# A two-layer encoder on one core: the clocks that give out weight splits follow each element, the fourth product of the seven goes onto the seventh's bank, the last block turns later, and two load slots are added

## The chip, the cores and the metric

The kernel runs on one core of one Trainium2 chip. The metric is device time in microseconds (us) of one execution, and less is better. Five engines work side by side, each through its own list of instructions in order: TensorE (PE: matmuls and transposes), VectorE (DVE), ScalarE (ACT), GpSimd (POOL) and SyncE (SP, which here starts nearly all transfers from memory). They wait for each other by semaphores.

## The reference

Two layers, each of three steps; after each step the sum with the step's input is normalised over 1024 features. The first and third steps are a gated feed-forward network (FFN), so there are four of these. The middle step is a bidirectional mLSTM in the first layer and a windowed attention in the second. All is float32, for 256 rows (two groups of 128, called t=0 and t=1).

```python
def swiglu(x, w_in, w_out):
    gu = x @ w_in                                   # (256,1024) @ (1024, 2*2816)
    g, u = gu[..., :D_FF], gu[..., D_FF:]
    return (jax.nn.silu(g) * u) @ w_out             # (256,2816) @ (2816,1024)

def reference(x, ffn_w_in, ffn_w_out, ln_g, ln_b, ...):
    for l in range(DEPTH):                          # DEPTH = 2
        x = layer_norm(ALPHA*x + 0.5*swiglu(x, ffn_w_in[l,0], ffn_w_out[l,0]), ln_g[l,0], ln_b[l,0])
        y = mlstm_mixer(x, ...) if l == 0 else window_attention(x, ...)
        x = layer_norm(ALPHA*x + y, ln_g[l,1], ln_b[l,1])
        x = layer_norm(ALPHA*x + 0.5*swiglu(x, ffn_w_in[l,1], ffn_w_out[l,1]), ln_g[l,2], ln_b[l,2])
    return x
```

## The kernel before

**Three matmuls for one.** Each float32 operand is split into a high part in TensorE's own format (`w_hi`, `xT_hi`) and the rest (`w_lo`, `xT_lo`); a product is hi*hi + hi*lo + lo*hi (`mm3`). So every piece of weights that arrives, 128 x 1024 numbers or 512 KB, is split before it is used: ACT casts the high part (`high`, "CAST w_hi"), DVE subtracts it from the raw piece (`low`, "TENSOR_TENSOR w_lo"). RING = 10 pieces can be split ahead of their use.

**An FFN.** The 2816 hidden columns go in blocks. First 512 columns "wide" (x is the stationary operand, the weights stream), then GROUPS = 3 groups, each of 256 columns "narrow" (the weights are stationary) and 512 columns whose gate and up-projection are made together in `seven`, a scheme of seven products instead of eight on 2 x 2 blocks. Its products use sums of x blocks (S1 to S4, made once by `x_sum`) and sums of weight blocks, which are made in place on DVE ("TENSOR_TENSOR s_raw") or by a transfer that adds onto what lies there (POOL, L204). Each product is 12 matmuls of 512 columns (`product`) onto a PSUM bank, and a closing function (`end1` to `end7`) takes the result out: copies on ACT (tile `e`), additions, subtractions and multiplications on DVE (tiles `e`), SiLU on ACT. `u0` and `u1` are the hidden values of t=0 and t=1; `tr` transposes them on TensorE ("MATMUL pw<-ident,e") and splits the result into `h_hi` and `h_lo` for the down-projection `down`, one row of 128 hidden columns of `w_out` at a time (12 matmuls "py").

Before the change the order in a group is: products 1 (bank qa), 2 (qc), a `down`, product 5 with S1 (qb), product 6 with S2 (onto qa, which is copied out first: `e1`), a `down`, product 3 with S4 (onto qb, copied out first as `e5`; `end3` makes `u0` by a subtraction and a multiplication), product 7 with S3 (onto qa, copied out first as `e2`; `end7` copies `e3` and subtracts into `u1`), in the first two groups a `down`, `tr` of `u0`, product 4 onto a fresh bank qd (`end4`: addition, SiLU, multiplication into `u1`), in the first two groups a `down`. The first two groups are "full"; the third, the last block, has no `down` at these two places. `tr` of `u1` comes in the middle of the next group's first narrow half, or, for the last block, inside `tail`.

**The end of an FFN.** `tail` does the last six down rows, first for t=0 and then for t=1, each in two halves of 512 columns, and norms each t as its sums are ready (`Norm.half`: "SCALAR_TENSOR_TENSOR x" and "BN_STATS"; `Norm.finish`: multiply by `ln_g`, add `ln_b`). `ln_g` and `ln_b` are loaded to two fixed tiles when g == 1.

**Transfers and slots.** A raw piece goes to one of 4 slots (`w_raw`), the blocks of `seven` that are summed to one of 6 more that exist only in an FFN (`s_raw`). A load is issued as soon as the instruction that frees its slot has been written, so SP waits for the DVE split that read the slot last.

**Who is given what, when.** In an FFN the planner `Paced` counts rough clocks (in ns) while the program is written: one for TensorE, one for DVE, one for ACT, one for transfers. After each matmul `fill` looks whether ACT or DVE is less than AHEAD = 900 ns ahead of TensorE's clock and, if the piece has been there for SOON (-600: 600 ns), writes one more split or sum into that engine's list. An engine's clock starts an instruction no earlier than its own clock and TensorE's; what other engines' results it needs is not followed, but for three tables of times of raw pieces and of their halves. So this planner's constants and costs set how many splits stand ahead of each `end` function in DVE's and ACT's lists. In the mixers the numbers of splits are written by hand.

All that goes through the planner's wrapper stands under L79 in the profile, so instructions are known by tiles: "w_hi", "w_lo", "e", "h_lo" and so on.

Of the kernel before, what the change touches and what calls it, by code (L numbers as in the profile page):

```python
# [1 line left out]

# [21 lines left out]
S_RAW = 6  # L24
RING = 10
# [11 lines left out]
AHEAD = 900.0  # L37
SOON = -600.0
LANDING = 2200.0
LOADING = 1340.0  # L40
ADDING = 8000.0


class Paced:
# [3 lines left out]
    def __init__(self, nc):  # L48
        self.nc = nc
        self.pe = self.vec = self.act = self.dma = 0.0  # L50
        self.filler = None
# [7 lines left out]
    def on_vector(self, name, n):  # L59
        self.vec = max(self.vec, self.pe) + (n + 71) / 0.96  # L60

    def on_scalar(self, name, n):
        self.act = max(self.act, self.pe) + n * 0.912 + 25

    def on_tensor(self, name, n):
        self.pe += 109.0 if name == "transpose" else n / 2.4 + 13.3
# [4 lines left out]
class Engine:  # L71
# [3 lines left out]
    def __getattr__(self, name):  # L75
        f = getattr(self.engine, name)

        def call(out, *args, **kw):
            r = f(out, *args, **kw)  # L79
            n = 1  # L80
            for d in getattr(out, "shape", (1, 1400))[1:]:
                n *= d
            self.told(name, n)
# [4 lines left out]
class Weights:  # L88
# [5 lines left out]
    def __init__(self, nc, pool, words, plan, after):  # L94
        self.nc, self.pool, self.words, self.plan, self.after = nc, pool, words, plan, after
        self.raw, self.parts, self.half, self.sums = {}, {}, [], []
        self.at, self.high_at, self.low_at = {}, {}, {}
        self.made = self.used = self.room = 0
        self.todo = {tag: [i for i, w in enumerate(words) if w["tag"] == tag] for tag in ("w_raw", "s_raw")}
        self.free = {"w_raw": RAW_BUFS, "s_raw": 0}  # L100
# [9 lines left out]
    def open(self, pool, end):  # L110

        self.spool, self.send = pool, end
        self.free["s_raw"] = S_RAW
        self.load()

    def load(self, most=None):
        nc = self.nc
        for tag, most_ in (("w_raw", most), ("s_raw", 1 if most is None else most)):
            n = 0
            while self.todo[tag] and self.free[tag] and (most_ is None or n < most_):  # L120
                i = self.todo[tag][0]
                if tag == "s_raw" and i >= self.send:
                    break
                pool = self.pool if tag == "w_raw" else self.spool
                t = pool.tile([128, D], F32, name=tag, tag=tag, bufs=RAW_BUFS if tag == "w_raw" else S_RAW)
                nc.sync.dma_start(t.rearrange("p (k f) -> p k f", k=self.words[i]["k"]), self.words[i]["src"])
                nc.dma = max(nc.dma, nc.pe + LANDING) + LOADING
                self.raw[i], self.at[i] = t, nc.dma
                self.free[tag] -= 1
# [3 lines left out]
    def drop(self, w):  # L133
        self.uses[w] -= 1
        if not self.uses[w]:
            del self.raw[w]
            self.free[self.words[w]["tag"]] += 1
# [7 lines left out]
    def high(self):  # L145
# [11 lines left out]
        nc.act = max(nc.act, self.at[p["word"]])  # L157
# [9 lines left out]
        self.high_at[i] = nc.act  # L167
# [3 lines left out]
    def low(self):  # L171
# [6 lines left out]
        nc.vec = max(nc.vec, self.high_at[i])  # L178
# [9 lines left out]
        self.low_at[i] = nc.vec  # L188
# [4 lines left out]
    def sum(self):  # L193
# [3 lines left out]
        if isinstance(v, int):  # L197
            nc.vec = max(nc.vec, self.at[w], self.at[v])
            nc.vector.tensor_add(t, t, self.raw[v])
            self.at[w] = nc.vec  # L200
            self.drop(v)
            self.load()
        else:
            nc.gpsimd.dma_start(t.rearrange("p (k f) -> p k f", k=self.words[w]["k"]), v, accum_op=OP.add)  # L204
            self.at[w] = max(nc.vec, nc.pe) + ADDING

    def fill(self):

        nc = self.nc
        while True:  # L210
            act, vec = max(nc.act, nc.pe), max(nc.vec, nc.pe)
            if act < nc.pe + AHEAD and len(self.half) < 2 and self.made < min(self.room, len(self.plan)):
                p = self.plan[self.made]
                if (p["word"] in self.raw and self.at[p["word"]] < act + SOON
# [3 lines left out]
            if vec < nc.pe + AHEAD:  # L218
                if self.half and self.high_at[self.half[0][0]] < vec + SOON:
                    self.low()  # L220
                    continue
                if self.sums and max(self.at[w] for w in self.sums[0][1:] if isinstance(w, int)) < vec + SOON:
# [4 lines left out]
    def take(self, n):  # L227
# [3 lines left out]
        self.nc.pe = max([self.nc.pe] + [self.low_at[j] for j in range(i, i + n)])  # L231
# [27 lines left out]
def trunk_kernel(ctx: ExitStack, tc: tile.TileContext, x, ffn_w_in, ffn_w_out, ln_g, ln_b, ml_w_in, ml_gate_b,  # L259
# [37 lines left out]
    def seven(w, c0, c1, downs):  # L297
# [70 lines left out]
    def load_x(t, h):  # L368
        s_ = slice(h * 512, h * 512 + 512)
        nc.sync.dma_start(xt[t][:, s_], x[0, t * 128:(t + 1) * 128, s_])  # L370
# [77 lines left out]
    def load_ln(l, n):  # L448
        t = []
        for name, w in (("g", ln_g), ("b", ln_b)):  # L450
            a = state.tile([128, D], F32, name="ln_" + name, tag="ln_" + name)
# [59 lines left out]
    def ffn(l, i, n, pending, last):  # L511
        with ExitStack() as ph:
# [3 lines left out]
            def h_room(width):  # L516
                return tuple(pool.tile([128, width, S], FR, name="h" + e, tag="h" + e, bufs=3) for e in ("_hi", "_lo"))
# [760 lines left out]
```

## Time and profile before

| | |
|---|---|
| time, three runs | 967.67 us median (964.8 to 967.9) |
| the profiled execution | 966.85 us, span of its instructions 965.1 us |
| TensorE | 931.9 us busy (97%), 4938 matmuls |
| DVE | 808.3 us (84%) |
| ACT | 550.0 us (57%) |
| transfers | 187.60 MB, 194 GB/s |
| granted TensorE clock, whole span | 0.992 |

The four FFNs lie at about 0 to 200, 310 to 495, 490 to 680 and 785 to 965 us of the span; the mLSTM lies between the first two, the attention between the last two. A matmul is reported as busy for longer than it keeps the next one off, since they overlap: rows in a row start closer together than the time that each shows. In the timeline a row gives the start, the time, the engine, the instruction with its output and inputs, and in brackets how long the engine was idle before it and what ended that.

### The profile page before, as it was taken

Reading aid. Unit: us, or ns where it says so; the run is one execution under the profiler, and the core shown is the slowest. Engines: PE = TensorE matmul, PEld = TensorE weight load, DVE = VectorE, ACT = ScalarE, POOL = GpSimd, SP = SyncE. Lnnn points to the kernel's source line nnn. Section 1 sums busy time; section 2 is a strip of 40 time slices with the busy share of each in tenths; the row PEclk is TensorE's granted clock in tenths of the full one; section 3 lists DMA queues with packets and bytes.
Section 4 is the critical chain, followed back from the end, with each engine's and each line's share of the span. In section 5 each row is a group of like instructions: output and inputs, shape, how many; then the busy total and the mean of one; then the engine's idle time right before and its main releaser. Section 6 shows DMA issues by size and latency. Waiting matters only on the chain.

```text
span 965.1 us, 13312 instructions
## 1 busy us (share of the span) xinstructions
PE 931.9 (97%) x4938; PEld 793.9 (82%) x4938; DVE 808.3 (84%) x925; ACT 550.0 (57%) x781; POOL 118.1 (12%) x194
## 2 busy tenths in 40 slices
PE   8999999899999999999999999998999999999996
PEld 6988788689988888989778888886888679898985
DVE  4897989797687888888898889897878898889886
ACT  4646565545654446566635475655468745666560
POOL 2010100020160100000010100000435310100001
PEclk9999999999999999999999999999999999999998
DMA  7949695545633858594657596856343356778541
GB/s 245 336 105 305 180 312 135 183 137 164 216 94 127 311 160 266 199 304 134 155 192 284 119 319 181 297 131 195 121 142 130 109 178 240 209 271 244 193 110 44
DMA packets 97697, 187.60 MB, mean 194 GB/s; under 512 B 5952, under 2 KB 36688, under 8 KB 97632
## 3 DMA queue, kind: packets, MB, share of 16 engines
q1 hardware_dynamic: 90880, 174.09, 53.2%
q0 software_dynamic: 6752, 12.66, 8.3%
q8 instruction: 39, 0.64, 0.3%
q14 instruction: 26, 0.21, 0.1%
HBM read 185.68 MB, written 1.05 MB: 193 GB/s over the span
## 4 chain that ended last, share of the span: by engine, by line
PE 67%; DVE 14%; DMA 8%; ACT 6%; issue 4%; POOL 1%; SPq 0%; ACTq 0%; DVEq 0%; POOLq 0%
PE pw L79 43%; PE py L79 24%; DVE w_lo L79 8%; DMA w_raw<-in_ffn_w_in_dram 4%; ACT w_hi L79 3%; DMA w_raw<-in_ffn_w_out_dram 3%; DVE s_raw L79 2%; DVE h_lo L79 1%; DVE x L79 1%; ACT e L79 1%; DVE e L79 1%; DVE S L79 1%; DMA w_raw<-in_at_w_in_dram 0%; DMA w_raw<-in_ml_w_in_dram 0%; ACT h_hi L79 0%
## 5 line engine op out<-in xcount | busy, mean ns | idle before, releaser
L79 DVE TENSOR_TENSOR w_lo<-w_raw,w_hi 128x1024 fp32r<-128x1024 f32 (+1 forms) x237 | 283.0, 1218 | 36.5 <-ACT w_hi L79 35.2
L79 ACT CAST w_hi<-w_raw 128x1024 fp32r<-128x1024 f32 (+1 forms) x237 | 241.0, 1048 | 111.0 <-DMA w_raw<-in_ffn_w_in_dram 64.4
L79 ACT CAST w_hi<-s_raw 128x1024 fp32r<-128x1024 f32 x144 | 149.7, 1050 | 104.8 <-DVE s_raw L79 81.3
L79 DVE TENSOR_TENSOR w_lo<-s_raw,w_hi 128x1024 fp32r<-128x1024 f32 x144 | 172.5, 1222 | 10.6 <-ACT w_hi L79 9.2
L79 PE MATMUL pw<-w_hi,xT_hi 128*128 128x512 f32 x368 | 147.2, 400 | 0.7 <-ACT xT_hi L79 0.7
L79 PE MATMUL pw<-w_lo,xT_hi 128*128 128x512 f32 x368 | 145.1, 394 | 2.0 <-DVE w_lo L79 2.0
L79 PE MATMUL pw<-w_hi,xT_lo 128*128 128x512 f32 x368 | 145.0, 394 | 1.0 <-DVE xT_lo L79 1.0
L79 PE MATMUL py<-w_hi,h_lo 128*128 128x512 f32 x352 | 138.3, 393 | 4.3 <-DVE h_lo L79 4.3
L79 PE MATMUL py<-w_hi,h_hi 128*128 128x512 f32 x352 | 138.5, 393 | 0.0
L79 PE MATMUL py<-w_lo,h_hi 128*128 128x512 f32 x352 | 138.0, 392 | 0.0
L79 PE MATMUL pw<-xT_hi,w_hi 128*128 128x256 f32 x448 | 127.8, 285 | 0.0
L79 PE MATMUL pw<-xT_hi,w_lo 128*128 128x256 f32 x448 | 126.7, 283 | 0.0
L79 PE MATMUL pw<-xT_lo,w_hi 128*128 128x256 f32 x448 | 126.7, 283 | 0.0
L204 POOL DMA_DIRECT2D s_raw<-in_ffn_w_in_dram x24 | 29.2, 1239 | 531.8 <-DVE w_lo L79 478.8
L79 DVE TENSOR_TENSOR s_raw<-s_raw 128x1024 f32<-128x1024 f32 x72 | 86.2, 1221 | 0.6
L79 PEld LDWEIGHTS pw<-xT_hi,w_hi 128*128 128x128 f32 x448 | 85.9, 192 | 0.5
L79 PEld LDWEIGHTS pw<-xT_lo,w_hi 128*128 128x128 f32 x448 | 85.9, 192 | 0.5
L79 PEld LDWEIGHTS pw<-xT_hi,w_lo 128*128 128x128 f32 x448 | 85.9, 192 | 0.0
L79 PEld LDWEIGHTS pw<-w_hi,xT_lo 128*128 128x128 f32 x368 | 69.9, 190 | 16.9 <-DVE xT_lo L79 1.8
L79 PEld LDWEIGHTS pw<-w_lo,xT_hi 128*128 128x128 f32 x368 | 70.1, 190 | 16.3 <-DVE w_lo L79 2.4
L79 PEld LDWEIGHTS py<-w_hi,h_lo 128*128 128x128 f32 x352 | 66.5, 189 | 20.1 <-DVE h_lo L79 6.2
L79 PEld LDWEIGHTS pw<-w_hi,xT_hi 128*128 128x128 f32 x368 | 70.0, 190 | 14.6 <-ACT xT_hi L79 1.1
(215 smaller groups left out, 1420.1 us busy)
## 6 DMA issues: line engine op xcount, KB each, us to landing
w_raw<-in_ffn_w_in_dram SPq DMA_DIRECT2D x104, 512.0 KB, 5.0
w_raw<-in_ffn_w_out_dram SPq DMA_DIRECT2D x88, 512.0 KB, 4.8
s_raw<-in_ffn_w_in_dram SPq DMA_DIRECT2D x72, 512.0 KB, 6.7
s_raw<-in_ffn_w_in_dram POOLq DMA_DIRECT2D x24, 512.0 KB, 6.5
w_raw<-in_ml_w_in_dram SPq DMA_DIRECT2D x24, 512.0 KB, 4.7
w_raw<-in_at_w_in_dram SPq DMA_DIRECT2D x12, 512.0 KB, 4.9
w_raw<-in_ml_w_out_dram SPq DMA_DIRECT2D x8, 512.0 KB, 4.1
w_raw<-in_at_w_out_dram SPq DMA_DIRECT2D x8, 512.0 KB, 3.9
```

Of the source, the lines that this page charges most:

```text
L79: r = f(out, *args, **kw)
L204: nc.gpsimd.dma_start(t.rearrange("p (k f) -> p k f", k=self.words[w]["k"]), v, accum_op=OP.add)
```

## The change

Five things, all in or for the FFNs:

1. `Paced` keeps for each tile an array with the time at which each element is there, and an instruction starts in the planner's count when its engine is free and its inputs are there (no longer "not before TensorE's clock"). A load's time has a new term SECOND. AHEAD goes from 900 to 300 and SOON from -600 to -1000. The three tables are gone. No instruction is added by this; it moves splits and sums in ACT's, DVE's and POOL's lists, and loads in SP's.
2. Product 4 goes onto bank qa, on top of product 7, and no longer onto its own bank: the copy `e3` on ACT and the addition in `end4` on DVE are gone, and product 4 now has to wait until `end7`'s subtraction has read the bank. `end4` is SiLU straight from the bank, then the multiplication.
3. Product 7 (S3) now comes ahead of product 3 (S4). In full groups `tr` of `u0` stays behind the `down` that follows; in the last block it moves behind product 4. So between product 3 and `tr` of `u0` lies one product's worth of matmuls everywhere (the `down`, or product 4); before it was two in a full group (product 7 and the `down`) and one in the last block (product 7).
4. Two slots `v_raw` are added in an FFN for ordinary pieces of that same FFN. The room comes from the hidden tiles (two buffers of width 4 and one of width 2 instead of three of width 4) and from the two tiles of `ln_g` and `ln_b`, which now go to freed `s_raw` slots at the FFN's end, just ahead of `tail` (in the mixers to tiles of their own at the old place).
5. In the plan of weight sums, the sum for product 7 (`b12 += b22`) comes right after the splits of product 6, and the splits for products 7 and 3 are in the new order.

```diff
-AHEAD = 900.0
-SOON = -600.0
+AHEAD = 300.0
+SOON = -1000.0
+SECOND = 1250.0
...
-    def on_vector(self, name, n):
-        self.vec = max(self.vec, self.pe) + (n + 71) / 0.96
+    def when(self, *aps):
+        t = 0.0
+        for ap in aps:
+            a = self.there.get(ap.name)
+            if a is not None:
+                i = self.place(ap)
+                t = max(t, a[i[i < a.size]].max(initial=0.0))
+        return t
...
+    def load(self, ap, source):
+        self.nc.sync.dma_start(ap, source)
+        come = self.pe + LANDING
+        alone, self.alone = self.alone, come > self.dma
+        self.dma = max(self.dma, come) + LOADING + (SECOND if alone and not self.alone else 0.0)
+        self.mark(ap, self.dma)
+
+    def on_vector(self, name, n, out, ins):
+        self.vec = max(self.vec, self.when(*ins)) + (n + 71) / 0.96
+        for o in out:
+            self.mark(o, self.vec + 115)
...
-            while self.todo[tag] and self.free[tag] and (most_ is None or n < most_):
+            while self.todo[tag] and (most_ is None or n < most_):
                 i = self.todo[tag][0]
-                if tag == "s_raw" and i >= self.send:
+                local = i < self.send
+                in_ = tag if self.free[tag] and (local or tag == "w_raw") else "v_raw"
+                if not self.free[in_] or in_ == "v_raw" and not (local and tag == "w_raw"):
                     break
...
         for j, a in enumerate(at(512, c0)):
-            after[s6[j]] = [(b11[j], a)]
+            after[s6[j]] = [(b11[j], a), (b12[j], b22[j])]
         downs(1)
-        s3 = [split_of(w_) for w_ in b22]
-        for j in range(2):
-            after[s3[j]] = [(b12[j], b22[j])]
-        [split_of(w_, None, p) for w_, p in zip(b12, s3)]
+        [split_of(w_, None, p) for w_, p in zip(b12, s6)]
+        for w_ in b22:
+            split_of(w_)
...
                 def end7():
-                    v["g1"] = copied(qa, "e3")
                     nc.vector.tensor_sub(v["u1"], v["u1"], qa)
 
                 def end4():
-                    nc.vector.tensor_add(v["g1"], v["g1"], qd)
-                    nc.scalar.activation(v["g1"], v["g1"], AF.Silu)
+                    v["g1"] = temp("g1")
+                    nc.scalar.activation(v["g1"], qa, AF.Silu)
                     nc.vector.tensor_mul(v["u1"], v["g1"], v["u1"])
...
+                product(qa, sum_("S3"), False, end7)
                 product(qb, sum_("S4"), False, end3)
-                product(qa, sum_("S3"), False, end7)
                 if full:
                     down(1)
-                qd = wbank()
-                tr(hB, 0, v["u0"])
-                product(qd, of(4, 1), True, end4)
+                    tr(hB, 0, v["u0"])
+                product(qa, of(4, 1), False, end4)
                 if full:
                     down(1)
+                else:
+                    tr(hB, 0, v["u0"])
...
-                if g == 1:
-                    gb = load_ln(l, n)
...
             nc.filler = None
+            gb = load_ln(lambda name: pool.tile([128, D], F32, name=name, tag="s_raw", bufs=S_RAW), l, n)
```

The matmuls are the same in number and kind. The three places below are those of which the prediction speaks; the numbers behind a tile's name tell its uses apart, and `x3` means three alike in a row.

VectorE, the last block of the first FFN, before: from the addition of `end2` (its first row) to the split `h_lo` of `u0`'s turn; `e_1565` is `u0`, `e_1543` is `u1`.

```order
L79 TENSOR_TENSOR e_1489<-e_1489,pw 128x512
L79 TENSOR_TENSOR s_raw<-s_raw 128x1024 x2
L79 TENSOR_TENSOR w_lo<-s_raw,w_hi 128x1024 x4
L79 TENSOR_TENSOR w_lo<-w_raw,w_hi 128x1024 x3
L79 TENSOR_TENSOR e_1565<-pw,e_1565 128x512
L79 TENSOR_TENSOR e_1565<-e_1489,e_1565 128x512
L79 TENSOR_TENSOR w_lo<-w_raw,w_hi 128x1024
L79 TENSOR_TENSOR e_1543<-e_1543,pw 128x512
L79 TENSOR_TENSOR h_lo<-pw,h_hi 128x4x128
```

The same place now; `e_1563` is `u0`, `e_1545` is `u1`, `g_1657` the SiLU of `end4`.

```order
L128 TENSOR_TENSOR e_1483<-e_1483,pw 128x512
L128 TENSOR_TENSOR w_lo<-s_raw,w_hi 128x1024 x6
L128 TENSOR_TENSOR w_lo<-w_raw,w_hi 128x1024 x4
L128 TENSOR_TENSOR e_1545<-e_1545,pw 128x512
L128 TENSOR_TENSOR w_lo<-w_raw,w_hi 128x1024 x2
L128 TENSOR_TENSOR e_1563<-pw,e_1563 128x512
L128 TENSOR_TENSOR e_1563<-e_1483,e_1563 128x512
L128 TENSOR_TENSOR w_lo<-w_raw,w_hi 128x1024
L128 TENSOR_TENSOR e_1545<-g_1657,e_1545 128x512
L128 TENSOR_TENSOR h_lo<-pw,h_hi 128x4x128
L128 TENSOR_TENSOR w_lo<-w_raw,w_hi 128x1024 x3
```

The two sums have gone ahead of `end2`; `end7`'s subtraction stands ahead of `end3`'s pair, with two splits between them.

ScalarE, the second group of the first FFN, before: from the copy `e1` (its first row) to the SiLU of `end6`; `e_1109` is the copy `e5`, `e_1133` the copy `e2`.

```order
L79 COPY e_1045<-pw 128x512
L79 CAST w_hi<-s_raw 128x1024 x4
L79 COPY e_1109<-pw 128x512
L79 CAST w_hi<-w_raw 128x1024
L79 COPY e_1133<-pw 128x512
L79 ACTIVATE e_1045<-e_1045 128x512
```

The same place now; `e_1096` is the copy `e5`, `e_1114` the copy `e2`.

```order
L128 COPY e_1038<-pw 128x512
L128 CAST w_hi<-s_raw 128x1024
L128 CAST w_hi<-w_raw 128x1024
L128 CAST w_hi<-s_raw 128x1024
L128 COPY e_1096<-pw 128x512
L128 CAST w_hi<-s_raw 128x1024 x2
L128 COPY e_1114<-pw 128x512
L128 ACTIVATE e_1038<-e_1038 128x512
```

One cast fewer, and only two of summed blocks where there were four, stand between the copies `e1` and `e5`.

ScalarE, the start of the program, before: the second row is the first piece of weights (in halves), the fourth has the next pieces, and the fifth the second half of x for both t.

```order
L79 CAST xT_hi<-py 128x4x128
L79 CAST w_hi<-w_raw 128x512 x2
L79 CAST xT_hi<-py 128x4x128
L79 CAST w_hi<-w_raw 128x1024 x3
L79 CAST xT_hi<-py 128x4x128 x2
L79 CAST w_hi<-w_raw 128x1024 x5
```

The same place now.

```order
L128 CAST xT_hi<-py 128x4x128
L128 CAST w_hi<-w_raw 128x512 x2
L128 CAST xT_hi<-py 128x4x128
L128 CAST w_hi<-w_raw 128x1024
L128 CAST xT_hi<-py 128x4x128 x2
L128 CAST w_hi<-w_raw 128x1024 x5
```

Two of the three casts of weights ahead of x's second half have gone behind it.

More of the change, by code (lines that the diff above doesn't have):

```diff
@@ L57, in __getattr__, with place, mark, on_scalar @@
         return getattr(self.nc, name)
-    def on_vector(self, name, n):
-        self.vec = max(self.vec, self.pe) + (n + 71) / 0.96
[L62 to L66, printed above, removed]
+    def place(self, ap):
+        f = ap.ap[0][0]
+        key = (ap.offset % f if f else 0, tuple(ap.ap[1:]))
+        if key not in self.places:
+            i = np.array([key[0]])
+            for step, n in key[1]:
+                i = (i[:, None] + step * np.arange(n if step else 1)[None, :]).reshape(-1)
+            self.places[key] = i
+        return self.places[key]
+    def when(self, *aps):
[6 more added lines that the diff above has]
+        return t
+    def mark(self, ap, t):
+        i = self.place(ap)
+        a = self.there.get(ap.name)
+        if a is None or a.size <= i.max():
+            self.there[ap.name] = np.zeros(int(i.max()) + 1)
+            if a is not None:
+                self.there[ap.name][:a.size] = a
+        self.there[ap.name][i] = t
+    def load(self, ap, source):
[8 more added lines that the diff above has]
+            self.mark(o, self.vec + 115)
+    def on_scalar(self, name, n, out, ins):
+        self.act = max(self.act, self.when(*ins)) + n * 0.912 + 25
+        for o in out:
+            self.mark(o, self.act + 125)
+    def on_tensor(self, name, n, out, ins):
+        self.pe = max(self.pe, self.when(*ins)) + (109.0 if name == "transpose" else n / 2.4 + 13.3)
+        for o in out:
+            self.mark(o, self.pe + 200)
         if self.filler is not None:
@@ L76, in __getattr__ @@
         f = getattr(self.engine, name)
+        if name.startswith("preload"):
+            return f
         def call(out, *args, **kw):
             r = f(out, *args, **kw)
[L80 to L83, printed above, removed]
+            ins = [x for x in [*args, *kw.values()] if hasattr(x, "ap")]
+            outs = [out] + ([kw["accum_out"]] if "accum_out" in kw else [])
+            size = lambda x: int(np.prod(x.shape[1:]))
+            self.told(name, size(out) if name in ("matmul", "transpose") else max(map(size, [out] + ins)), outs, ins)
             return r
@@ L112, in open @@
         self.spool, self.send = pool, end
[L113 removed]
+        self.free["s_raw"], self.free["v_raw"] = S_RAW, V_RAW
         self.load()
@@ L218, in fill @@
             if vec < nc.pe + AHEAD:
-                if self.half and self.high_at[self.half[0][0]] < vec + SOON:
+                if self.half and nc.when(self.half[0][1]) < vec + SOON:
                     self.low()
                     continue
-                if self.sums and max(self.at[w] for w in self.sums[0][1:] if isinstance(w, int)) < vec + SOON:
+                if self.sums and nc.when(*(self.raw[w] for w in self.sums[0][1:] if isinstance(w, int))) < vec + SOON:
                     self.sum()
```

47 lines of the change are left out of this document (21 added, 26 removed).

## The prediction

> **What bounds the kernel now.** I read the page first, then who TensorE waited for, then a table by stretches for its clock, then the timeline at each of the long waits.
>
> ```profile
> span 965.1 us, 13312 instructions
> PE 931.9 (97%) x4938; PEld 793.9 (82%) x4938; DVE 808.3 (84%) x925; ACT 550.0 (57%) x781; POOL 118.1 (12%) x194
> ```
>
> TensorE is the bound: it is idle for 965.1 - 931.9 = 33.2 us, and the change adds and removes no matmul. So the change can only return idle time, and time in which matmuls run slowly. The waits of TensorE, longest in total first (total, times, longest):
>
> ```profile
> PE pw L79 <- DVE e L79: 6.4, 4, 3.4
> PE py L79 <- DVE h_lo L79: 4.3, 3, 2.0
> PE pw L79 <- ACT e L79: 2.5, 5, 0.9
> PE pw L79 <- DVE hh L79: 2.4, 2, 2.1
> PE pw L79 <- DVE w_lo L79: 2.0, 1, 2.0
> ...
> PE pw L79 <- ACT xT_hi L79: 0.7, 1, 0.7
> ```
>
> These six belong to the FFNs, where the lists are changed, and sum to 18.3 us. The table by stretches gives the length, TensorE's busy time and the granted clock:
>
> ```profile
> 0.00:21.00 21.00, 16.18 (x63) 0.92 0.72 230
> 165.00:195.00 30.00, 25.98 (x111) 0.94 0.63 189
> 320.00:465.00 145.00, 142.43 (x777) 1.00 0.73 227
> ...
> 650.00:685.00 35.00, 31.92 (x139) 0.95 0.47 151
> ```
>
> Three stretches with long waits have a clock below 1. What that costs is busy time by the missing share: 16.18 x 0.08 + 25.98 x 0.06 + 31.92 x 0.05 = 1.3 + 1.6 + 1.6 = 4.5 us. So at most 18.3 + 4.5 = 22.8 us can come back.
>
> **The change part by part.**
>
> *The last block's turn.* First FFN, TensorE and then DVE (the wait stands in brackets):
>
> ```profile
> 177.66 0.63 PE L79 MATMUL pw<-ident,e 128*128 128x128 f32 x4 [3.38 <-DVE e L79]
> ...
> 172.69 3.50 DVE L79 TENSOR_TENSOR w_lo<-w_raw,w_hi 128x1024 fp32r<-128x1024 f32 x3 [0.72 <-ACT w_hi L79]
> 176.11 0.68 DVE L79 TENSOR_TENSOR e<-pw,e 128x512 f32<-128x512 f32 x1
> 176.83 0.69 DVE L79 TENSOR_TENSOR e<-e,e 128x512 f32<-128x512 f32 x1
> ```
>
> TensorE stands from 174.3, the end of the seventh product, to 177.66; the turn of u0 has to wait until DVE, busy with three splits, has made u0 (177.52). Now two sums stand ahead of `end2` that stood behind it, so ten splits (at 3.50 / 3 = 1.17 us) and one addition (0.68) lie between `end2` and `end7`: 12.4 us. In that time TensorE does down, S1, S2, down and S3, five products. One product is 12 matmuls, 2.72 us by the second row here:
>
> ```profile
> 120.73 5.76 PE pw L79 x24
> 126.49 2.72 PE py L79 x12
> ```
>
> Five are 13.6 us, so DVE reaches `end7` 1.2 us early unless it waits for ACT. From S3's end it then has 0.68 + 2 x 1.17 = 3.0 us to `end3`, whose product ends after 2.7 us, and u0 is ready 0.3 + 0.68 + 0.69 = 1.7 us behind that product's end. Product 4 (2.72 us) lies between, so the turn has 1.0 us to spare. I take back the whole 6.4 us of the first wait row, of which this is more than half.
>
> *The removed copy and addition.* Their rows, by tile (minimum, median, maximum in ns):
>
> ```profile
> L79 ACT COPY e<-pw x48: 569/578/594, 63.7 to 937.9; 128x512 f32<-128x512 f32 x48
> L79 DVE TENSOR_TENSOR e<-e,pw x36: 678/682/689, 66.0 to 943.3; 128x512 f32<-128x512 f32 x36
> ```
>
> Twelve copies at 0.58 and twelve additions at 0.68 go, 6.9 us of ACT and 8.2 us of DVE; neither engine is the bound, so this counts only as slack: nothing by itself. What product 4 gains in return is a wait for `end7`'s subtraction, which stands first behind S3 in DVE's list; product 4 comes 2.7 us behind S3 in a last block and 5.4 and a turn in a full group, so I cost it at nothing. If it waits, all of TensorE's list waits with it, and ACT's SiLU for that.
>
> *Products 3 and 7 against their copies.* Second group, first FFN, ACT and then TensorE:
>
> ```profile
> 118.01 2.19 ACT L79 CAST w_hi<-s_raw 128x1024 fp32r<-128x1024 f32 x2 [3.29 <-DVE s_raw L79]
> 120.10 0.58 ACT L79 COPY e<-pw 128x512 f32<-128x512 f32 x1
> ...
> 120.73 0.50 PE L79 MATMUL pw<-w_hi,S_hi 128*128 128x512 f32 x1 [0.56 <-ACT e L79]
> ```
>
> The copy of a bank is late since two casts ahead of it waited 3.29 us for sums on DVE. The sums now come ahead of `end2` and those casts behind the copy (the order of ScalarE above), and a `down` lies between S2 and the next product onto either bank. All of the 2.5 us should go.
>
> *The tail.* Second FFN, DVE and then TensorE:
>
> ```profile
> 483.32 2.35 DVE L79 TENSOR_TENSOR w_lo<-w_raw,w_hi 128x1024 fp32r<-128x1024 f32 x2
> 485.84 2.53 DVE L79 TENSOR_TENSOR w_lo<-w_raw,w_hi 128x1024 fp32r<-128x1024 f32 x2 [0.17 <-ACT w_hi L79]
> 489.62 0.68 DVE L79 TENSOR_TENSOR h_lo<-pw,h_hi 128x512 fp32r<-128x512 f32 x1
> ...
> 490.35 0.50 PE L79 MATMUL py<-w_hi,h_lo 128*128 128x512 f32 x1 [1.70 <-DVE h_lo L79]
> ```
>
> Four splits, x's sum and its statistics lie ahead of u1's `h_lo`. Now three splits stand there, and the addition of `end4` (0.68) is gone: DVE is about 1.2 + 0.7 = 1.9 us earlier. That covers the 1.70 here and nearly the longest of the three (2.0). I take 3.5 of the 4.3 us.
>
> *The start.* TensorE's transposes of x's second half, ACT, and TensorE's first matmuls on it:
>
> ```profile
> 10.41 1.36 PE L79 MATMUL py<-ident,x 128*128 128x128 f32 x8 [0.23 <-DMA x<-in_x_dram]
> ...
> 12.39 1.05 ACT L79 CAST w_hi<-w_raw 128x1024 fp32r<-128x1024 f32 x1 [1.85 <-DMA w_raw<-in_ffn_w_in_dram]
> 14.71 1.06 ACT L79 CAST xT_hi<-py 128x512 fp32r<-128x512 f32 x2
> ...
> 15.34 0.50 PE L79 MATMUL pw<-w_hi,xT_hi 128*128 128x512 f32 x1 [0.69 <-ACT xT_hi L79]
> 17.79 0.79 PE L79 MATMUL pw<-w_lo,xT_hi 128*128 128x512 f32 x1 [1.95 <-DVE w_lo L79]
> ```
>
> x's second half, turned by 11.8, was cast only at 14.71, behind pieces of weights that were still landing. Ahead of them it is cast by 11.8 + 1.06 = 12.9, the piece that lands at 12.39 by 13.9, and that piece is split by 15.1 (1.17 for a split). TensorE would be there at about 14.6 (0.69 before 15.34) and wait some 0.5 us for the split. Of 0.7 + 2.0 I take 2.2 us.
>
> *The start of the second FFN* (DVE, then TensorE):
>
> ```profile
> 342.46 0.68 DVE L79 TENSOR_TENSOR hh<-sg,pw 128x512 f32<-128x512 f32 x1
> ...
> 343.29 0.63 PE L79 MATMUL pw<-ident,hh 128*128 128x128 f32 x4 [2.07 <-DVE hh L79]
> ```
>
> One split of a summed block is moved from ahead of `hh` to behind it, 1.2 us of the 2.4.
>
> *The clock.* With the waits, the slow stretches behind them go: 4.0 of 4.5 us. The row is the 0.94 around the 3.38 us wait. [...]
>
> *Slots and ln.* Six loads ahead instead of four cost no engine anything; I give them nothing. The two `ln` loads now stand in SP's list behind the next stage's fifth piece.
>
> ```profile
> DMA to landing us min/median/max: 4.3/5.2/6.1
> ...
> ln_b<-in_ln_b_dram SPq DMA_DIRECT2D x6, 512.0 KB, 6.6
> ```
>
> Issued at about the end of product 4, they land 5 to 7 us later. `ln_g` is wanted behind t=0's half of the tail (six rows of 6 matmuls, as many as 3 products, 8.2 us) and x's sums, some 3 us later than it lands. Nothing.
>
> *New waits in the full groups.* Here u0's turn has one product behind it where it had two. Two full groups of before, DVE's subtraction and multiplication for u0:
>
> ```profile
> 125.89 0.69 DVE L79 TENSOR_TENSOR e<-pw,e 128x512 f32<-128x512 f32 x1
> 126.61 0.69 DVE L79 TENSOR_TENSOR e<-e,e 128x512 f32<-128x512 f32 x1
> ...
> 371.87 5.73 PE pw L79 x24
> ...
> 378.70 0.69 DVE L79 TENSOR_TENSOR e<-e,e 128x512 f32<-128x512 f32 x1
> ```
>
> Product 3 ended 2.9 us into the rows of 24 matmuls, at 123.6 and 374.7; u0 was ready at 127.3 and 379.4, so 3.7 and 4.65 us behind. One product gives 2.7. With DVE as late as that, each turn would pay 1.0 to 1.9 us; with the reckoning of the last block (1.7), none. That reckoning is nearest to what the new lists say, but it has only 1.0 us to spare and no wait of DVE for ACT in it, so I put 0.3 us on each of the 12 turns, 3.6 us (from 0 to 12 x 1.9 = 22.8).
>
> Sum: 6.4 + 2.5 + 3.5 + 2.2 + 1.2 + 4.0 = 19.8 returned, 3.6 paid, 16.2 net. The profiled execution took 966.85 us (1.75 more than its span), so 950.65; the median of the runs shown is 0.8 us above it. I say 951.
>
> **The rivals.**
>
> *DVE is as late at every turn as it was* (15%). For it: the two groups above are full ones that the planner made, and 84% of DVE is busy. Against it: it let splits run 900 ns ahead of TensorE, now 300. At the middle of 1.0 and 1.9, 12 x 1.45 = 17.4 in place of 3.6: 966.85 - 19.8 + 17.4 = 964.4.
>
> *The boundaries stay as they were* (15%): the next stage's pieces and the `ln` loads compete, so the tail, `hh` and one slow stretch (3.5 + 1.2 + 1.4 = 6.1) don't come back: 956.7. For it: at 485.84 DVE waited for a cast in the tail already. Against it: `ln` has some 3 us.
>
> *Slower* (9%): product 4 has given up its own bank, so a late DVE now stops TensorE twice in a block, first at product 4 for `end7`'s subtraction and then at the turn. It decides where DVE reaches `end7` over 2.0 us late (2.7 less the subtraction). If each of the 12 turns pays what the worst of the shown groups would pay, 1.9, and each of the four last blocks 1 us more at product 4, it is 22.8 + 4 = 26.8 against 19.8: 973.9. For it is the wait row of 0.56 above, a product that stands still for the copy of its bank. [...] Against: the subtraction now stands first in the list behind S3.
>
> *The change does little of what it says* (6%): gains and new waits cancel, 967.
>
> **How the numbers follow.** The forecast, 944 to 957, has 55%; the rivals 15, 15, 9 and 6. A measurement of this kernel tells 0.3%, 2.9 us, from no change. All of the forecast, the boundary case and a good half of the late-DVE case (below 964) are faster: 0.55 + 0.15 + 0.10 = 0.80; the rest of that case and the last one are the same, 0.11; slower 0.09. The range goes from 942 (all 22.8 back, few new waits: 966.85 - 22.8 = 944, and 2 us of small waits not listed) to 964, where the late-DVE case lies; what is left out is the upper half of that case and the last two, and a little below.
>
> **What would show it.** Right: TensorE's waits for DVE `e` under 3 us in all, for ACT `e` and for `h_lo` nearly gone; the first wait for `w_lo` under 1 us; the clock 1.00 from 165 to 195. Wrong: waits of 1 us or more before `pw<-ident,e` in full groups; a wait of a product of xT for DVE's `e` (the bank); DVE waiting for `ln_g`; idle time of TensorE that is again about 33 us.

## The result and the profile after

The changed kernel took 950.53 us (median of 4 runs, 949.59 to 951.61) beside 967.38 us for the kernel before: a ratio of 0.9831, with a 95% interval of 0.9810 to 0.9852. The forecast was 951. The profiled execution took 951.61 us, the longest of the four. Its page begins:

```profile
span 949.9 us, 13274 instructions
...
PE 926.9 (98%) x4938; PEld 793.5 (84%) x4938; DVE 796.8 (84%) x913; ACT 543.4 (57%) x769; POOL 117.5 (12%) x194
```

The span is 15.2 us shorter. TensorE's idle time fell from 33.2 to 23.0 us, and its busy time by 5.0 us for the same 4938 matmuls. Part of this is clock: ahead of the last matmul, the trace of before has three stretches of 3.41 us with a granted clock of 0.50 (from 17.76, 178.19 and 676.53 us), each of which loses 1.7 us, and this one has one (from 334.33 us), so 3.4 of the 5.0. The rest is not accounted for; busy time differs by 3.1 us (924.8 to 927.9) between e4, e8 and e12 below, with a granted clock of 0.998, 0.997 and 0.998 over the span. What TensorE waits for now (total, times, longest):

```profile
PE pw L128 <- DVE hh L128: 5.0, 3, 3.4
PE pw L128 <- DVE xT_lo L128: 1.5, 3, 0.6
...
PE pw L128 <- DVE w_lo L128: 1.3, 2, 0.7
PE py L128 <- DMA x<-in_x_dram: 1.1, 1, 1.1
...
PE py L128 <- ACT h_hi L128: 0.6, 2, 0.3
```

The rows for DVE `e` (6.4), ACT `e` (2.5), DVE `h_lo` (4.3) and ACT `xT_hi` (0.7) are gone. The row for `hh` has doubled, from 2.4 to 5.0. The same four stages by stretches (length, TensorE busy, clock):

```profile
0.00:21.00 21.00, 18.41 (x79) 15.18 (x80) 10.63 (x14) 10.99 (x14) 6.38 (x15) 1.00 0.81 259
158.00:188.00 30.00, 30.00 (x137) 24.68 (x136) 24.92 (x28) 14.22 (x17) 1.88 (x2) 1.00 0.53 176
310.00:455.00 145.00, 141.50 (x769) 123.40 (x769) 126.22 (x127) 85.06 (x102) 7.30 (x6) 0.99 0.72 228
638.00:673.00 35.00, 34.72 (x160) 28.20 (x160) 28.40 (x32) 17.17 (x21) 1.87 (x2) 1.00 0.47 163
```

The two stretches with a tail are filled (30.00 of 30.00 and 34.72 of 35.00 us) at full clock; 25.98 of 30.00 at 0.94 and 31.92 of 35.00 at 0.95 stood there before. The third has lost a little, behind the longest wait for `hh`. The last block's turn in the first FFN, DVE and then TensorE:

```profile
169.72 0.69 DVE L128 TENSOR_TENSOR e<-pw,e 128x512 f32<-128x512 f32 x1
170.44 0.69 DVE L128 TENSOR_TENSOR e<-e,e 128x512 f32<-128x512 f32 x1
```

```profile
172.04 0.60 PE L128 MATMUL pw<-ident,e 128*128 128x128 f32 x4
```

DVE has made `u0` at 171.13, TensorE turns it at 172.04 with no idle time in brackets; it was 3.38 us before. In all 12 blocks `u0` is ready about 1.85 us behind the end of product 3 (2.27 in the last) and the turn starts 0.45 to 0.9 us later without a wait.

### The profile page after: what moved, and what is told of

It reads as the page before. It is cut to its first block, busy times and chain, and to the rows that moved or that the text cites. A ratio compares the mean times of both kernels' runs of the same rounds, so it can differ in the third digit from the quotient of the medians.

```text
span 949.9 us, 13274 instructions
## 1 busy us (share of the span) xinstructions
PE 926.9 (98%) x4938; PEld 793.5 (84%) x4938; DVE 796.8 (84%) x913; ACT 543.4 (57%) x769; POOL 117.5 (12%) x194
## 4 chain that ended last, share of the span: by engine, by line
PE 79%; DVE 7%; DMA 6%; ACT 3%; issue 3%; POOL 1%; SPq 0%; POOLq 0%; DVEq 0%; ACTq 0%
PE pw L128 48%; PE py L128 30%; DVE w_lo L128 4%; DMA s_raw<-in_ffn_w_in_dram 3%; DMA w_raw<-in_ffn_w_in_dram 1%; DMA w_raw<-in_ffn_w_out_dram 1%; ACT w_hi L128 1%; ACT sc L128 1%; DVE x L128 1%; DMA x<-in_x_dram 1%; ACT xT_hi L128 0%; DVE s_raw L128 0%; SPq L94 0%; DVE o L128 0%; DVE hh L128 0%
## 5 line engine op out<-in xcount | busy, mean ns | idle before, releaser
L128 DVE TENSOR_TENSOR w_lo<-w_raw,w_hi 128x1024 fp32r<-128x1024 f32 (+1 forms) x237 | 281.7, 1218 | 19.4 <-ACT w_hi L128 18.1
L128 ACT CAST w_hi<-s_raw 128x1024 fp32r<-128x1024 f32 x144 | 146.9, 1049 | 65.0 <-DVE s_raw L128 32.5
```

## The experiments

The kernel before took 964.0 to 964.7 us beside these runs and 967.4 beside the changed kernel, so ratios are compared, not times; 1% is 9.65 us. The changed kernel's ratio rests on those four runs at 967.4, and by the medians in us every run below compares about 0.3% better with it than by the ratios. "Order" stands for parts 2, 3 and 5 of the change (product 4 on the seventh's bank, the order of products with the later last turn, the plan of sums), "clocks" for part 1, "slots" for part 4, which has two halves: two slots, and `ln` loaded just ahead of the tail.

| run | what it has | us | ratio to before, 95% | TensorE idle | TensorE busy |
|---|---|---|---|---|---|
| changed kernel | clocks, order, slots, late ln | 950.5 | 0.9831 (0.9810 to 0.9852) | 23.0 | 926.9 |
| e1 | clocks | 968.0 | 1.0037 (1.0019 to 1.0055) | 32.6 | 932.3 |
| e2 | order | 977.6 | 1.0131 (1.0105 to 1.0157) | 39.8 | 938.9 |
| e3 | clocks, order, late ln | 961.1 | 0.9968 (0.9951 to 0.9984) | 27.5 | 932.8 |
| e4 | changed, hh first | 951.7 | 0.9859 (0.9836 to 0.9881) | 24.0 | 926.2 |
| e5 | slots, late ln | 958.5 | 0.9936 (0.9916 to 0.9957) | 28.0 | 927.7 |
| e6 | clocks, slots, late ln | 962.8 | 0.9981 (0.9962 to 1.0000) | 30.6 | 930.3 |
| e7 | order, slots, late ln | 976.6 | 1.0121 (1.0099 to 1.0144) | 41.9 | 935.3 |
| e8 | clocks, order | 951.0 | 0.9852 (0.9829 to 0.9875) | 20.5 | 927.9 |
| e9 | changed, last turn early | 958.5 | 0.9939 (0.9921 to 0.9957) | 29.7 | 927.9 |
| e10 | changed, own bank | 970.6 | 1.0077 (1.0048 to 1.0106) | 33.8 | 935.5 |
| e11 | changed, old limits | 956.8 | 0.9925 (0.9895 to 0.9955) | 25.6 | 930.8 |
| e12 | changed, slots later | 946.3 | 0.9816 (0.9789 to 0.9844) | 19.1 | 924.8 |

**e1, the clocks alone.** The changed file with the order, the slots and `ln` put back:

```diff
-V_RAW = 2
+V_RAW = 0
...
-            after[s6[j]] = [(b11[j], a), (b12[j], b22[j])]
+            after[s6[j]] = [(b11[j], a)]
...
+                    v["g1"] = copied(qa, "e3")
...
-                product(qa, of(4, 1), False, end4)
+                product(qd, of(4, 1), True, end4)
```

> The new clocks with their two limits, on the old order of products, the old plan of sums, product 4 on its own bank with its copy and addition, no extra slots, ln at its old place. My theory (both parts are needed: the last block's turn waits because only one product lies behind product 3, whatever the clocks say) expects the start (2.2 us), the tail (2.5) and little else: about 962 us, with TensorE still waiting 4 us or more for DVE e. Rival 'the clocks are the whole change': 951. Rival 'the clocks do nothing by themselves': 967.

Measured 1.0037: not faster. My 962 was too low by 6 us, and the wait for DVE `e` was 0.3 us, not 4: the last blocks' turns come without a wait although they and the products stand as before the change. A new wait had come instead, in the tails. First TensorE's wait, then DVE in the second FFN's tail:

```profile
PE py L128 <- DVE w_lo L128: 7.7, 8, 2.2
```

```profile
468.07 0.68 DVE L128 TENSOR_TENSOR e<-e,pw 128x512 f32<-128x512 f32 x1
469.45 0.69 DVE L128 TENSOR_TENSOR e<-e,e 128x512 f32<-128x512 f32 x1 [0.70 <-ACT e L128]
470.06 3.49 DVE L128 TENSOR_TENSOR w_lo<-w_raw,w_hi 128x1024 fp32r<-128x1024 f32 x3
```

The old closing of product 4 goes from DVE (addition) to ACT (SiLU) and back to DVE (multiplication); the split of the row that TensorE wants next stands behind it.

**e2, the order alone.** The kernel before with the hunks of parts 2, 3 and 5 as the diff above has them:

```diff
-                product(qb, sum_("S4"), False, end3)
                 product(qa, sum_("S3"), False, end7)
+                product(qb, sum_("S4"), False, end3)
...
-                product(qd, of(4, 1), True, end4)
+                product(qa, of(4, 1), False, end4)
```

> The old clocks and limits with the new order of products, the new plan of sums, product 4 on the seventh's bank and the later last turn; no extra slots, ln at its old place. My theory expects the last block's turn back (6.4 us of waits and 1.6 of slow clock at the first FFN) and part of the copies' 2.5, but not the start: about 957. Rival 'the clocks are the whole change': 967. Rival 'the order is the whole change': 951. Rival of the prediction, a late DVE at every full group's turn (there is one product behind product 3 now, and the old clocks let DVE run late): above 967, with waits of 1 us or more before pw<-ident,e.

Measured 1.0131, with e7 the slowest. The place is none that I named. TensorE's wait in total, DVE and then ACT in the last FFN:

```profile
PE pw L79 <- ACT e L79: 12.4, 4, 3.5
```

```profile
839.62 1.22 DVE L79 TENSOR_TENSOR s_raw<-s_raw 128x1024 f32<-128x1024 f32 x1
```

```profile
840.92 2.00 ACT L79 CAST w_hi<-s_raw 128x1024 fp32r<-128x1024 f32 x2 [3.07 <-issue]
...
846.14 0.58 ACT L79 COPY e<-pw 128x512 f32<-128x512 f32 x1
```

ACT's two casts start right behind a sum that DVE ends at 840.84 (the profile names no releaser, so that they wait for it is read from the times). Behind them stand a copy, three more casts and the copy `e2` at 846.14, for which product 7 waits 3.5 us. So in each FFN's first group the product behind this copy waits, 12.4 us in all; the granted clock over the span is 0.982, where the kernel before has 0.992 (busy time 938.9 and 931.9). With the new clocks the planner follows when the sum ends, and the casts are written behind the copy. In the changed kernel the same copy waits for TensorE alone:

```profile
818.17 0.59 ACT L128 COPY e<-pw 128x512 f32<-128x512 f32 x1 [2.13 <-PE pw L128]
...
819.18 2.94 ACT L128 CAST w_hi<-s_raw 128x1024 fp32r<-128x1024 f32 x3
```

**e3, the changed kernel without the two slots** (`ln` still late).

```diff
-V_RAW = 2
+V_RAW = 0
```

> The changed kernel without the two extra slots. My theory gives them nothing: 950.5 within 1 us. A narrower form of it: the two extra loads stand ahead of the blocks for the sums in SP's queue at the start of the second FFN, ACT's cast waits for them (6.1 us idle at 329) and x's sums and hh stand behind that cast, so without the slots the gap of 3.57 us at 331 is 2 us shorter or more: 948.5. Rival 'the slots carry the gain': 955 or more, with new waits for w_lo or w_hi.

Measured 0.9968, 1.4% behind the changed kernel: the rival's number, though not its waits for `w_lo` or `w_hi`. The narrower form held for its wait, not for its time: the waits for `hh` fell from 5.0 to 0.5 us. The largest loss is in the tails, 5.8 us of waits for `h_lo`: ACT, then DVE, then TensorE in that of the second FFN.

```profile
479.61 1.05 ACT L128 CAST w_hi<-w_raw 128x1024 fp32r<-128x1024 f32 x1 [3.87 <-DMA w_raw<-in_ffn_w_in_dram]
```

```profile
480.69 1.23 DVE L128 TENSOR_TENSOR w_lo<-w_raw,w_hi 128x1024 fp32r<-128x1024 f32 x1 [3.69 <-ACT w_hi L128]
481.83 0.68 DVE L128 SCALAR_TENSOR_TENSOR x<-x,py 128x512 f32<-128x512 f32 x1
...
483.15 0.68 DVE L128 TENSOR_TENSOR h_lo<-pw,h_hi 128x512 fp32r<-128x512 f32 x1
```

```profile
483.88 0.80 PE L128 MATMUL py<-w_hi,h_lo 128*128 128x512 f32 x1 [1.96 <-DVE h_lo L128]
484.48 0.63 PE L128 MATMUL py<-w_hi,h_hi 128*128 128x512 f32 x1
484.90 0.63 PE L128 MATMUL py<-w_lo,h_hi 128*128 128x512 f32 x1
```

A piece of the next stage lands late, its split stands ahead of x's sums and `h_lo`, and TensorE stands. Behind the wait its matmuls start 0.42 us apart (484.48 to 484.90; the granted clock from 470 to 485 is 0.94); in the changed kernel, where the clock from 462 to 492 is 1.00, it is 0.23 (487.69 to 487.92).

**e8, no slots and ln at its old place** tells whose fault that is. With the loads, the hidden tiles get their three buffers back:

```diff
-V_RAW = 2
+V_RAW = 0
...
-                tag, n_ = ("h", 2) if width == 4 else ("hc", 1)
...
+                if g == 1:
+                    gb = load_ln(lambda name: state.tile([128, D], F32, name=name, tag=name), l, n)
...
-            gb = load_ln(lambda name: pool.tile([128, D], F32, name=name, tag="s_raw", bufs=S_RAW), l, n)
```

> The run without slots, and ln loaded at the second group into tiles of its own as in the kernel before (hidden tiles of three buffers again). The prediction's 'ln costs nothing': 961 within 1 us. Rival 'the two ln loads ahead of the tail keep the last pieces back' (3.87 us of waiting for a piece in the tail of the second FFN; two loads are 2 x 1.3 us in each of three tails): 955 to 957, with that wait under 1.5 us. Then the slots are worth only what is left, about 5 us.

Measured 0.9852, even better than the rival's 955, and not to be told from the changed kernel. So without slots the late `ln` and the smaller room of the hidden tiles together cost about 1.2% (e8 against e3, 11 us), and the slots repay it. No run parts these two; that it is `ln` is read from the waits. How, SP's list shows, in the second FFN's tail: e3 first, then the changed kernel.

```profile
465.95 3.96 SPq L94 DMA_DIRECT2D w_raw<-in_ffn_w_in_dram  x3
469.96 0.46 SPq L494 DMA_DIRECT2D ln_g<-in_ln_g_dram  x1
...
473.30 9.01 SPq L94 DMA_DIRECT2D w_raw<-in_ffn_w_in_dram  x5
```

```profile
461.58 6.83 SPq L94 DMA_DIRECT2D w_raw<-in_ffn_w_in_dram  x5
468.46 0.47 SPq L494 DMA_DIRECT2D ln_g<-in_ln_g_dram  x1
...
471.93 3.03 SPq L94 DMA_DIRECT2D w_raw<-in_ffn_w_in_dram  x3
```

With three pieces of the next stage ahead of `ln`, five come behind it and too late for the tail; with five ahead, three. This holds in all ten runs with a late `ln`: with three ahead in the second and third FFN (e3, e6, e10), TensorE waited 5.8, 3.8 and 3.6 us for `h_lo`; with four to six (the changed kernel, e4, e5, e7, e9, e11, e12), 0.5 us or nothing.

**e4, hh written ahead of x's first two sums.**

```diff
-                            if t == 1 and a % 2:
-                                [[None, lambda: x_raw(0), None, lambda: x_raw(1)], [None, x_one, None, x_two]][m][a]()
+                            if t == 1 and m == 0 and a % 2:
+                                x_raw(a // 2)
...
                     b_mul(sg, ps[1])
+                x_one()
+                x_two()
```

> The changed kernel with x's first two sums (S1, S2) written behind the multiplication that makes hh of t=1, in the three later FFNs. My theory: hh is late because it stands in DVE's list behind the low part of S2, which waits for ACT, whose cast waits for a transfer; the 5.0 us of waits for hh go and nothing comes for it, since S1 is wanted two narrow halves, two down rows and two products later: 946. Rival 'hh is late because the product it reads is' or 'the next wait takes its place': 950.

Measured 0.9859, no gain. The cause that I gave is right for `hh`, whose waits fell from 5.0 to 0.9 us, but 3.3 us of waits for ACT `e` appeared; the copy of a bank now stood behind casts that waited for a sum on DVE:

```profile
542.40 1.99 ACT L128 CAST w_hi<-s_raw 128x1024 fp32r<-128x1024 f32 x2 [3.60 <-DVE s_raw L128]
544.30 0.58 ACT L128 COPY e<-pw 128x512 f32<-128x512 f32 x1
```

**e5, e6, e7: the slots with nothing else, with the clocks, with the order.** Each adds to the kernel before, e1 or e2 (with the room of the hidden tiles and the `load` of part 4):

```diff
+V_RAW = 2
...
-                if g == 1:
-                    gb = load_ln(l, n)
...
+            gb = load_ln(lambda name: pool.tile([128, D], F32, name=name, tag="s_raw", bufs=S_RAW), l, n)
```

> The kernel before with only the two slots and what makes room for them (the hidden tiles, ln loaded ahead of the tail). The runs so far: clocks alone 968.0, order alone 977.6, both without slots 961.1, all 950.5 to 951.7. New theory: the slots carry the tails by themselves (a cast in a tail waited 3.87 us for a piece, and h_lo and x's sums stood behind it), and cost the waits for hh at the starts of the later FFNs: 964.7 - 10.4 = 954.3, h_lo waits under 2 us, hh waits over 4 us. Rival 'the three parts only work together': 962 to 967, with the h_lo waits of the kernel before (4.3 us).

> The changed kernel with the old order of products, the old plan of sums, product 4 on its own bank and the earlier last turn. If the slots are worth as much here as with the new order: 968.0 - 10.4 = 957.6. If the order costs or gives nothing once the slots are there: 951. If slots need the new order: 966.

> The kernel before with the slots and the new order of products and sums, the bank and the later last turn; the old clocks. If the slots are worth as much here: 977.6 - 10.4 = 967.2, with TensorE's 12.4 us of waits for ACT e still there (those stood at the product behind S2, not in a tail). If those waits came from pieces that landed late: 955.

Measured 0.9936, 0.9981 and 1.0121. e5 fell between theory and rival: `h_lo` 0.5 and `hh` 5.0 us as the theory said, but 6 us are what is left of 10. It also has no wait for DVE `e` left, of 6.4 before, with the old clocks and the old order. In e6 and e7 the slots bring about 5 and 1 us, and e7 keeps its waits for ACT `e` (15.1 us). With the slots as without them the order is worth something only with the clocks: without slots clocks and order cost 0.4% and 1.3% each alone, and bring 1.5% together (e8); with slots the order costs 1.9% without the clocks (e7 against e5) and brings 1.5% with them (changed kernel against e6).

**e9, the last block's turn back ahead of product 4.**

```diff
-                    tr(hB, 0, v["u0"])
+                tr(hB, 0, v["u0"])
                 product(qa, of(4, 1), False, end4)
...
-                else:
-                    tr(hB, 0, v["u0"])
```

> The changed kernel with the last block's turn of u0 ahead of product 4, straight behind product 3. u0 is ready 1.85 us behind that product's end in every block of the changed kernel, and the turn comes 0.5 us behind it at the soonest, so TensorE waits some 1.4 us in each of four FFNs, and more where DVE is late: 956 to 958 (the prediction's 6.4 us). Rival 'the order of products 3 and 7 alone saves the last block': 951.

Measured 0.9939, 1.1% behind the changed kernel, as the theory said. Here no product lies between product 3 and the turn, where the kernel before had product 7. One wait in each FFN:

```profile
PE pw L128 <- DVE e L128: 8.0, 4, 2.3
```

**e10, product 4 on its own bank again.**

```diff
                 def end7():
+                    v["g1"] = copied(qa, "e3")
                     nc.vector.tensor_sub(v["u1"], v["u1"], qa)
...
-                product(qa, of(4, 1), False, end4)
+                product(qd, of(4, 1), True, end4)
```

> The changed kernel with product 4 on a bank of its own again, so with the copy on ACT and the addition on DVE in each of 12 blocks. The prediction's 'removed at nothing': 951 within 1 us. Rival 'the freed 0.6 us of each engine is what makes the turns and the tail fit': waits for e and h_lo, 955 or more. Rival 'sharing the bank costs a wait of product 4': 949 or less.

Measured 1.0077, 2.5% behind the changed kernel: my "nothing" is the miss of this study. TensorE's waits, then DVE, ACT and TensorE in the second FFN's tail:

```profile
PE py L128 <- ACT h_hi L128: 7.8, 5, 1.7
```

```profile
470.17 2.35 DVE L128 TENSOR_TENSOR w_lo<-w_raw,w_hi 128x1024 fp32r<-128x1024 f32 x2
472.44 0.68 DVE L128 TENSOR_TENSOR e<-e,pw 128x512 f32<-128x512 f32 x1
```

```profile
473.16 0.63 ACT L128 ACTIVATE e<-e 128x512 f32<-128x512 f32 x1 [4.37 <-DVE e L128]
473.69 0.57 ACT L128 CAST h_hi<-pw 128x512 fp32r<-128x512 f32 x1
```

```profile
474.31 0.50 PE L128 MATMUL py<-w_hi,h_hi 128*128 128x512 f32 x1 [1.72 <-ACT h_hi L128]
```

Product 4 ends at about 470.4, but DVE reaches the addition only at 472.44, behind two splits; ACT waits 4.37 us for it, and the cast of `h_hi` for u0's turn, which TensorE wants next, stands behind ACT's SiLU. All four tails have this wait of 1.72 us. In the changed kernel ACT waits for TensorE alone there:

```profile
467.99 0.60 ACT L128 ACTIVATE g<-pw 128x512 f32<-128x512 f32 x1 [1.91 <-PE pw L128]
```

In e10 also only three pieces stand ahead of `ln`, in the second and third FFN, as in e3, and the waits for `h_lo` follow. By the two traces the span is 19.4 us longer, 10.8 of it idle and 8.6 busy. In 10 us from each of 172, 482, 660 and 940 the granted clock is 0.83, which loses 1.7 us each, 6.8 of the 8.6; in the changed kernel it is 1.00 in all four tails.

**e11, the old limits with the new clocks.**

```diff
-AHEAD = 300.0
-SOON = -1000.0
+AHEAD = 900.0
+SOON = -600.0
```

> The changed kernel with AHEAD and SOON as before (900 and -600), the clocks still tracking each element. The prediction put DVE's being on time down to AHEAD: then splits stand 0.6 us more ahead of each end function, waits of about 1 us come before the turns, 955 to 960. Rival 'the tracking does it, not the limits': 951 within 1 us.

Measured 0.9925, within the range given for my theory, but at another place, by TensorE's waits:

```profile
PE pw L128 <- DVE hh L128: 7.6, 3, 3.2
...
PE pw L128 <- DVE e L128: 1.2, 3, 0.7
```

The turns wait 1.2 us in all, and `hh` costs 7.6. The prediction's reason fails: the old limits don't make the turns late, and neither do the old clocks with the new order (1.1 us of waits for DVE `e` in e2, 0.3 in e7). The limits matter at the FFN's start. The tracking matters for the copies: e7 is this run with the old clocks, with 15.1 us of waits for ACT `e` where this one has none, and 976.6 us.

**e12, the slots opened only ahead of the first seven products.**

```diff
-        self.free["s_raw"], self.free["v_raw"] = S_RAW, V_RAW
+        self.free["s_raw"], self.free["v_raw"] = S_RAW, 0
...
                     x_rest()
+                    W.free["v_raw"] = V_RAW
+                    W.load()
```

> The changed kernel with the two slots opened only ahead of the first seven products of each FFN. The slots cost the waits for hh (5.0 us with them from the start, 0.5 and less in both runs of these clocks without them) and pay in the tails for the later ln loads: both from two loads that are issued earlier. Opened later they should pay without costing: 946, hh waits under 1 us and h_lo waits under 1 us. Rival 'lateness only moves' (as when hh was put first: 951.7, with new waits for ACT e): 950 to 952.

Measured 946.3 us, 0.9816. The waits for `hh` and `h_lo` are both gone from the trace, whose span is 943.9 us, 6.0 us less than the changed kernel's, with 19.1 us idle and a granted clock of 0.998 where the changed kernel has 0.996. Clearly faster than the kernel before; by the timed ratio its interval overlaps that of the changed kernel, so that it beats it is shown by one trace each and not by the ratios; the times, 945.6 to 946.9 beside 949.6 to 951.6, point the same way.

## Why the prediction was right, and where its reasons were not

**The last block's turn (6.4 us): right that it goes, wrong about why.** I put it down to the products that lie around the turn. But the wait also goes with the products as they were: 0.3 us with the clocks alone (e1), none with the slots alone (e5). What made `u0` late before was not the number of splits only. In the 3.38 us case ACT had waited for a piece that landed late, and DVE behind it for ACT (1.24 and 0.72 us):

```profile
169.66 1.05 ACT L79 CAST w_hi<-s_raw 128x1024 fp32r<-128x1024 f32 x1 [1.42 <-DMA s_raw<-in_ffn_w_in_dram]
```

In e5 ACT has no such wait and DVE has the same instructions in the same order between `end2` and `end3`, and the turn comes on time. So each of three parts removes this wait by itself (e2, the order alone, has 1.1 us left, in a full group). e1 pays elsewhere, 7.7 us for `w_lo` in the tails. e9 shows that in the new order, with product 7 ahead of product 3, the turn must stand behind product 4 (8.0 us); it doesn't show that this move returned the 6.4.

**The copies of banks (2.5 us): right in size,** by the mechanism named, with one thing left out: the order without the new clocks makes them worse (12.4 us in e2), and the tracking turns this round (e11 against e7).

**The removed copy and addition ("nothing by itself"): wrong.** I reasoned that neither engine is the bound, and counted the addition's 0.68 us only in the tail. But the addition is a step in the chain from product 4 to the last turn, and DVE reaches it behind two splits. e10 puts the two instructions back in each block and pays 20 us by the times, 24 by the ratios: 7.2 more of waits for `h_hi`, 3.6 for `h_lo`, and most of the rest (6.8) in clock. In a tail, where no `down` is left to cover, a step on another engine counts with what is queued ahead of it.

**The tail (3.5 us, 4.3 measured): right in size, for half of the reason.** Fewer splits ahead of `h_lo` was what I named; what sets how many have been done by then is whether their pieces have landed (in e3 a cast there waited 3.87 us for one). The changed kernel's DVE in the second FFN's tail now waits for ACT, and ACT for TensorE (4.63 us ahead of that cast):

```profile
477.16 0.69 DVE L128 TENSOR_TENSOR h_lo<-pw,h_hi 128x512 fp32r<-128x512 f32 x1 [1.70 <-ACT h_hi L128]
```

**Slots and `ln` ("nothing"): right as a sum on top of the clocks and the order, wrong in both parts.** The late `ln`, with the room for it, costs some 11 us there and the slots repay it (e3, e8). On the kernel before the same part alone brings 6 us (e5). I asked only when `ln` is wanted, and not who is queued behind it: five pieces, in e3.

**The start of the later FFNs (1.2 us back): wrong sign.** `hh` costs 2.6 us more. ACT, DVE and TensorE at the second FFN's start:

```profile
328.94 1.05 ACT L128 CAST w_hi<-s_raw 128x1024 fp32r<-128x1024 f32 x1 [6.10 <-DMA s_raw<-in_ffn_w_in_dram]
329.90 0.61 ACT L128 CAST S_hi<-S 128x512 fp32r<-128x512 f32 x1
```

```profile
330.54 0.69 DVE L128 TENSOR_TENSOR S_lo<-S,S_hi 128x512 fp32r<-128x512 f32 x1 [4.99 <-ACT S_hi L128]
...
333.79 0.68 DVE L128 TENSOR_TENSOR hh<-sg,pw 128x512 f32<-128x512 f32 x1
```

```profile
334.62 1.09 PE L128 MATMUL pw<-ident,hh 128*128 128x128 f32 x4 [3.41 <-DVE hh L128]
```

The step that failed is that I costed one moved split, and the two loads more at nothing. They go ahead of the blocks for the sums; the planner writes ACT's cast of such a block although it has not landed, the cast waits 6.10 us, and `S_hi`, `S_lo` and `hh` stand in a row behind it. e3, e8 and e12, in which the slots open later or never, have 0.5 us or less.

**New waits in full groups (3.6 us paid): 0.** The reckoning of 1.7 us was right (1.85); the late-DVE rival did not occur. My argument against it, the 300 ns, was not the reason: with 900 ns these waits are 1.2 us in all (e11).

**The start (2.2 us):** the waits for `xT_hi` and `w_lo` of 2.7 us went; 1.3 us of waits for `w_lo` came at the first group's sums and 0.5 at x's transfer, so 0.9 net. **The clock (4.0 us): right in size.** Busy time fell by 5.0, of which 3.4 are clock. The three slow stretches of before cost 5.1 us (3 x 3.41 x 0.50) rather than 4.5: TensorE was busy for 3.38 to 3.42 us of each, and the prediction took the missing share of a longer stretch from its busy part alone.

By the waits and the busy time 6.4 + 2.5 + 4.3 + 0.9 - 2.6 + 5.0 = 16.5 us, against 16.2 forecast and 15.2 of span measured; smaller waits make up the rest. That the number came so close is luck: two errors cancelled, since the 3.6 us charged for the turns did not come and `hh` came out 3.8 us worse than forecast, and a term that I put at nothing, the copy and the addition, carries the others. Only the runs show whose the gain is: the clocks and the order with the bank bring all of it together (e8), the slots with late `ln` bring 0.6% alone (e5) and nothing on top of the two. The rival that gave up bank makes TensorE stop did not decide: no product waited for `end7`'s subtraction.

Open is why the limits matter for `hh` (e11), and whether e12 with `ln` at its old place gains more; neither was tried. Nor was the shared bank tried on the old order of products.

## What to carry to other kernels

Ask of each small operation in which chain it stands and what is queued ahead of it on its engine, not whether that engine is the bound: 0.6 us of copy and 0.7 us of addition, taken out of a chain in each of 12 blocks, were worth 2% here, with what the planner moved for them. A load that is moved costs what stands behind it in its queue (11 us in e3 against e8, with the room for it), and a slot helps or hurts by what the earlier load overtakes (in e5 the waits for `h_lo` fell from 4.3 to 0.5 us, those for `hh` rose from 2.4 to 5.0). Parts of a schedule can each be slower alone and faster together, so a part is to be tried both on the old kernel and taken out of the new one.

## What the runs showed of the hardware

In e10 the same wait of 1.72 us for `h_hi` stands in each of the four tails; 10 us around it by stretches, the second FFN first, then the first, third and fourth:

```profile
471.00:481.00 10.00, 8.15 (x38) 6.13 (x37) 8.04 (x9) 4.05 (x5) 0.00 (x0) 1.00 0.83 282
...
172.00:182.00 10.00, 8.15 (x28) 5.92 (x27) 9.30 (x11) 5.20 (x6) 0.00 (x0) 0.83 0.92 307
660.00:670.00 10.00, 8.15 (x28) 5.90 (x27) 7.55 (x8) 4.04 (x5) 0.00 (x0) 0.83 0.92 286
940.00:950.00 10.00, 8.16 (x30) 6.05 (x29) 6.23 (x8) 1.10 (x2) 0.00 (x0) 0.83 0.00 0
```

TensorE is as busy in all four, but does 38 matmuls in one and 28 to 30 in the others. The granted clock is 1.00 in the one and 0.83 in the others, which over 10 us loses 1.7 us: there the clock lost as much again as the wait of 1.72 us was long, and behind the same wait in the second FFN's tail nothing. The kernel before has both cases too: 1.3 us behind the end of a wait of 1.97 us for `h_lo` (at 675.22) the clock fell to 0.50 for 3.41 us, while behind the wait of 2.07 us for `hh` (at 343.29) it stayed 1.00, as all the way from 181.60 to 676.53 us. So in these traces the length of a wait alone does not tell whether it costs clock; what does was not shown.
